# Gates and half of a convolution's columns taken out of the attention and projection stages and made 2x2 block products of seven

## The chip, the cores and the metric

One Trainium2 chip, one of its cores. The metric is the device time of one execution in microseconds (us); for the kernel before it is the median of three runs. The engines are named as in the profile: PE is TensorE (PEld its weight loads), DVE VectorE, ACT ScalarE, POOL GpSimd, SP the queue that issues nearly all DMAs.

## What is computed

One decoder layer over 1024 positions of width 1024, in float32. A normalised input h is multiplied by one wide matrix w_in; its columns feed three token mixers (an mLSTM with 4 heads, a gated convolution of width 3, a stick-breaking attention with 16 heads) and three sets of gate columns. Then follow projections, a sum under the gates, an output product and an MLP of width 4096.

```python
h = rmsnorm(x, norm_mix_g)
ml_q, ml_k, ml_v, ml_o, ml_i, ml_f, sc_b, sc_c, sc_u, sb_q, sb_k, sb_v, g_ml, g_sc, g_sb = split(h @ w_in)
y_ml = head_rmsnorm(sigmoid(ml_o) * mlstm(ml_q, ml_k, ml_v, ...), ml_norm_g)
y_sc = sc_b * causal_conv3(sc_c * sc_u, conv_w)
y_sb = stick_breaking(sb_q, sb_k, sb_v)   # a = sigmoid(z_ts) * prod_{s<j<t} (1 - sigmoid(z_tj))
merged = (sigmoid(g_ml) * (y_ml @ w_ml_proj) + sigmoid(g_sc) * (y_sc @ w_sc_proj)
          + sigmoid(g_sb) * (y_sb @ w_sb_proj))
x = x + merged @ w_out
x = x + square(relu(rmsnorm(x) @ w_up)) @ w_down
return rmsnorm(x)
```

## The kernel before

**Products.** Every large product is made of three matmuls (`mm3`, lines 129 to 132): each operand is split into a high and a low part (`split`, an ACT copy in line 136 and a DVE subtraction in line 137), and high x high, high x low and low x high are added up in a PSUM bank. `dense_ws` (line 159) gives 128 columns of h @ w for all 1024 positions: it loads 512 KB of weights into a tile `wr`, splits them (two ACT and two DVE instructions of 128x512), and issues 2 x 8 x 3 = 48 matmuls of 512 columns into two banks. `dense_as` (line 173) does the same with the positions as stationary operand and 256 columns: 192 matmuls.

**Stages.** (1) The normalised, transposed input `hT` is made, 16 pairs of high and low tiles of 128x512. (2) mLSTM: for each head `ml_proj` and `ml_attn`. (3) Attention: for p = 0 to 7 (two heads each), `sb_qk` (K and Q, two `dense_ws`), `sb_attn`, and `sc_unit(p)`, which is 128 columns of the convolution (three `dense_ws`: c, u, b); before each even p `sb_v` makes the values of a pair of p's (one `dense_as`). (4) `branch` three times: eight columns of 128 of a projection, each with a `gate` before it (a `dense_ws` with a sigmoid). (5) w_out. (6) The MLP, which already works with 2x2 blocks of seven products (Strassen-Winograd): the up stage takes 16 units of 84 matmuls each.

**Attention's chain.** For each of 24 tiles of scores in one p (12 of them 512 wide, four each 384, 256 and 128; 16 lie on the diagonal): two score matmuls (lines 556 and 557); two sigmoids on ACT (559, 560); on POOL, for the tile on the diagonal, two selects (564, 566), for others a copy (570); a running product on DVE, the scan (572); a product on POOL (573); transposes on PE (590); splits on ACT and DVE (136, 137); matmuls with the values (603 to 607); a copy and an add into the output (613, 614). The tiles come in four groups, G = 3 to 0, of 8, 8, 4 and 4. K of the next p needs tiles that this p gives back after G = 2 (line 620).

**Order.** A scheduler lays out each engine's queue when the program is built. `ml_attn` and `sb_attn` are marked as urgent (`tc.high_priority(offset=AHEAD)`); the `dense_ws` of the convolution, of the next K and Q and of the next values stand between attention's instructions wherever the scheduler finds the latter not ready. Each engine works through its queue in order.

The lines that the change touches most:

```python
    for p in range(8):                       # 687
        ...
        Q, T = sb_qk(p)
        with tc.high_priority(offset=AHEAD):
            sb_attn(p, Q, T, vt)
        ...
        sc_unit(p)                           # 695
```

Of the kernel before, what the change touches and what calls it, by code (L numbers as in the profile page):

```python
# [16 lines left out]
P = 128  # L17
# [17 lines left out]
AHEAD = 2000  # L35


@with_exitstack
def hybrid_block_kernel(
# [66 lines left out]
    def g(name):  # L106
        return rings[name].get()
# [517 lines left out]
    def sc_unit(ct):  # L625
        cs, zs = [None, None], [None, None]

        def ev_c(th, ps):
            cs[th] = g("sc")
            nc.scalar.activation(cs[th][:, :512], ps, AF.Copy)  # L630

        def ev_u(th, ps):
            z = g("sc")
            zs[th] = z
            if th == 0:
                nc.gpsimd.memset(z[:, 0:2], 0.0)
            else:
                nc.gpsimd.tensor_copy(z[:, 0:2], zs[0][:, 512:514])
            nc.vector.tensor_tensor(z[:, 2:514], cs[th][:, :512], ps, ALU.mult)
            t = cs[th]  # L640
            nc.vector.tensor_scalar(t[:, :512], z[:, 2:514], cw[:, 2, ct:ct + 1], None, ALU.mult)
            nc.vector.scalar_tensor_tensor(t[:, :512], z[:, 1:513], cw[:, 1, ct:ct + 1], t[:, :512], ALU.mult, ALU.add)
            nc.vector.scalar_tensor_tensor(t[:, :512], z[:, 0:512], cw[:, 0, ct:ct + 1], t[:, :512], ALU.mult, ALU.add)
            if th == 1:
                free(*zs)

        def ev_b(th, ps):
            t = cs[th]
            nc.vector.tensor_tensor(t[:, :512], t[:, :512], ps, ALU.mult)
            nc.sync.dma_start(ysc_d[ct][:, th * 512:(th + 1) * 512], t[:, :512])  # L650
            free(t)

        dense_ws(w_in, C_SCC + ct * P, hT, ev_c)
        dense_ws(w_in, C_SCU + ct * P, hT, ev_u)
        dense_ws(w_in, C_SCB + ct * P, hT, ev_b)
# [10 lines left out]
    def gate(c0, ct, ring=None):  # L666
        sg = [None, None]

        def ev_g(th, ps):
            sg[th] = (ring or ring_f).get()  # L670
            nc.scalar.activation(sg[th][:, :512], ps, AF.Sigmoid)
        dense_ws(w_in, c0 + ct * P, hT, ev_g)
        return sg
# [24 lines left out]
    unplan(ring_f, "u", "be", "yo", "avt", "sc")  # L698
    unplan(banks, "z", "av", "acc", "tp")
    plan(banks, acc=6, tp=2)  # L700

    def branch(i, w, c0, yd, sgs):
        y = [[None, None] for _ in range(KO)]
        nxt = len(sgs)
        for ko in range(KO):
            y[ko] = [(ring_r.get(), ring_r.get()) for _ in range(2)]
            load_split(yd[ko], 1, y[ko])
            if ko in (1, 3, 5) and nxt < (5 if i == 0 else 3):
                sgs[nxt] = gate(c0, nxt)
                nxt += 1  # L710
        for ct in range(KO):
            while nxt < min(KO, ct + 2):
                sgs[nxt] = gate(c0, nxt)
                nxt += 1
            if i == 2 and ct == KO - 1:
                free_all(hT)
            sg = sgs.pop(ct)

            def ev_p(th, ps):
                s = sg[th][:, :512]  # L720
                nc.vector.tensor_tensor(s, s, ps, ALU.mult)
                if i == 0:
# [403 lines left out]
```

## Time and profile before

| | |
|---|---|
| three runs | 2522.91 us median (2522.04 to 2523.82) |
| profiled execution | 2525.46 us, of it 2523.7 us span |
| busy | PE 98%, DVE 60%, ACT 44%, POOL 30% of the span |
| attention's scans (line 572) | first at 533.0 us, last at 1238.2 us |
| gates (line 671) | first sigmoid at 1222.4 us, last at 1738.9 us |
| products with the projections (line 721) | 1286.7 to 1761.2 us |
| output product (line 850) | 1782.8 to 1856.7 us |
| up stage (line 939) | 1874.3 to 2176.5 us |

A row of the timeline gives start, duration, engine, line, operation, output<-inputs and shape; "[0.95 <-POOL gf L570]" behind it says how long the engine had been idle and what released it. A row of groups ends in the number of instructions, busy time and mean duration. PE's matmuls are pipelined: one of 512 columns shows a duration of 397 ns, but the distance from one to the next is what counts.

### The profile page before, as it was taken

Reading aid. Unit: us, or ns where it says so; the run is one execution under the profiler, and the core shown is the slowest. Engines: PE = TensorE matmul, PEld = TensorE weight load, DVE = VectorE, ACT = ScalarE, POOL = GpSimd, SP = SyncE. Lnnn points to the kernel's source line nnn. Section 1 sums busy time; section 2 is a strip of 40 time slices with the busy share of each in tenths; the row PEclk is TensorE's granted clock in tenths of the full one; section 3 lists DMA queues with packets and bytes.
Section 4 is the critical chain, followed back from the end, with each engine's and each line's share of the span. In section 5 each row is a group of like instructions: output and inputs, shape, how many; then the busy total and the mean of one; then the engine's idle time right before and its main releaser. Section 6 shows DMA issues by size and latency. Waiting matters only on the chain.

```text
span 2523.7 us, 35184 instructions
## 1 busy us (share of the span) xinstructions
PE 2473.0 (98%) x12792; PEld 2086.4 (83%) x12792; DVE 1520.9 (60%) x2337; ACT 1115.0 (44%) x2270; POOL 751.7 (30%) x1108
## 2 busy tenths in 40 slices
PE   7999999999999999999999999999989999899998
PEld 6899898988888888888888888888868888678776
DVE  6465463767757767767621322424357677797996
ACT  6343333346546546546521311313446666643343
POOL 3000010034434334344300000000246565654563
PEclk9999999999999999999999999999999999999999
DMA  4121111122122122222221311312426665875663
GB/s 123 47 64 55 55 39 59 36 70 64 50 64 55 51 63 55 57 61 59 91 69 50 117 42 50 117 42 86 140 72 209 203 202 182 279 247 185 226 203 128
DMA packets 273637, 256.66 MB, mean 102 GB/s; under 512 B 20016, under 2 KB 224816, under 8 KB 273464
## 3 DMA queue, kind: packets, MB, share of 16 engines
q1 hardware_dynamic: 271016, 249.96, 31.7%
q10 hardware_dynamic: 2448, 4.46, 0.5%
q8 instruction: 100, 1.64, 0.3%
q14 instruction: 73, 0.60, 0.1%
HBM read 178.85 MB, written 67.13 MB: 97 GB/s over the span
## 4 chain that ended last, share of the span: by engine, by line
PE 89%; DVE 4%; POOL 2%; DMA 2%; issue 2%; ACT 1%; SPq 0%; POOLq 0%; DVEq 0%; ACTq 0%
PE ps L130 27%; PE ps L131 27%; PE ps L132 27%; PE ps L590 2%; DVE gr L137 1%; PE ps L557 1%; PE ps L556 1%; PE ps L607 1%; PE ps L606 1%; DVE gf L1081 1%; DMA gr<-gd 1%; DVE gf L572 1%; POOL gf L759 0%; DMA wr<-in_w_in_dram 0%; POOL gf L573 0%
## 5 line engine op out<-in xcount | busy, mean ns | idle before, releaser
L130 PE MATMUL ps<-gr,wh 128*128 128x512 f32 x1938 | 768.3, 397 | 7.5 <-ACT gf L939 6.7
L131 PE MATMUL ps<-gr,wh 128*128 128x512 f32 x1938 | 767.1, 396 | 0.0
L132 PE MATMUL ps<-gr,wl 128*128 128x512 f32 x1924 | 760.4, 396 | 0.0
L130 PEld LDWEIGHTS ps<-gr,wh 128*128 128x128 f32 x1938 | 365.0, 188 | 91.0 <-ACT gf L939 7.1
L131 PEld LDWEIGHTS ps<-gr,wh 128*128 128x128 f32 x1938 | 364.7, 188 | 83.3 <-DVE gr L137 0.6
L132 PEld LDWEIGHTS ps<-gr,wl 128*128 128x128 f32 x1924 | 362.0, 188 | 82.9
L137 DVE TENSOR_TENSOR wl<-wr,wh 128x512 fp32r<-128x512 f32 (+1 forms) x261 | 187.6, 726 | 302.1 <-ACT wh L136 297.7
L136 ACT ACTIVATE wh<-wr 128x512 fp32r<-128x512 f32 (+1 forms) x268 | 167.7, 631 | 434.7 <-PE ps L131 374.6
L130 PE MATMUL ps<-gr,gr 128*128 128x512 f32 (+3 forms) x730 | 261.1, 364 | 6.1 <-DVE gf L1081 5.8
L131 PE MATMUL ps<-gr,gr 128*128 128x512 f32 (+3 forms) x730 | 264.2, 364 | 0.0
L132 PE MATMUL ps<-gr,gr 128*128 128x512 f32 (+3 forms) x730 | 262.8, 364 | 0.6 <-DVE gr L1021 0.6
L572 DVE TENSOR_TENSOR_SCAN gf<-gf 128x512 f32<-128x512 f32 (+1 forms) x192 | 200.8, 1048 | 100.5 <-POOL gf L564 56.8
L137 DVE TENSOR_TENSOR gr<-gf,gr 128x512 fp32r<-128x512 f32 (+2 forms) x222 | 206.5, 942 | 62.9 <-ACT gr L136 58.8
L573 POOL TENSOR_TENSOR gf<-gf,gf 128x512 f32<-128x512 f32 (+1 forms) x192 | 185.3, 967 | 175.8 <-DVE gf L572 145.8
L130 PE MATMUL ps<-wh,gr 128*128 128x256 f32 (+2 forms) x792 | 229.3, 290 | 7.2 <-DVE gf L1081 4.1
L131 PE MATMUL ps<-wl,gr 128*128 128x256 f32 (+2 forms) x800 | 229.3, 287 | 0.0
L132 PE MATMUL ps<-wh,gr 128*128 128x256 f32 (+2 forms) x792 | 225.4, 288 | 0.2 <-DVE gr L140 0.2
L136 ACT ACTIVATE gr<-ps 128x256 fp32r<-128x256 f32 (+2 forms) x304 | 129.7, 442 | 170.7 <-PE ps L132 70.7
L759 POOL TENSOR_TENSOR gf<-wr,wr 128x512 f32<-128x512 f32 x22 | 34.6, 1572 | 563.6 <-PE ps L854 552.7
L759 POOL TENSOR_TENSOR gf<-gf,gf 128x512 f32<-128x512 f32 x106 | 152.5, 1445 | 118.8 <-ACT gf L953 90.1
L136 ACT ACTIVATE gr<-gf 128x512 fp32r<-128x512 f32 (+2 forms) x222 | 135.9, 622 | 109.6 <-POOL gf L759 71.8
L137 DVE TENSOR_TENSOR gr<-ps,gr 128x256 fp32r<-128x256 f32 (+2 forms) x304 | 142.7, 483 | 59.0 <-ACT gr L136 55.9
(204 smaller groups left out, 3969.6 us busy)
## 6 DMA issues: line engine op xcount, KB each, us to landing
wr<-in_w_in_dram SPq DMA_DIRECT2D x102, 512.0 KB, 3.7
gr<-gd SPq DMA_DIRECT2D x145, 256.0 KB, 5.1
gd<-gr SPq DMA_DIRECT2D x128, 256.0 KB, 2.5
wr<-in_w_down_dram SPq DMA_DIRECT2D x30, 512.0 KB, 5.2
gd<-gf SPq DMA_DIRECT2D x48, 256.0 KB, 2.6
gf<-in_w_up_dram SPq DMA_DIRECT2D x36, 256.0 KB, 3.0
gr<-gr SPq DMA_DIRECT2D x64, 128.0 KB, 2.2
gf<-in_x_dram SPq DMA_DIRECT2D x31, 256.0 KB, 3.7
```

Of the source, the lines that this page charges most:

```text
L130: mm(ps, lh, rh, start=start, stop=False, skip_group_check=chain)
L131: mm(ps, lh, rl, start=False, stop=False, skip_group_check=chain)
L132: mm(ps, ll, rh, start=False, stop=stop, skip_group_check=chain)
L136: nc.scalar.activation(hi, src, AF.Copy)
L137: nc.vector.tensor_tensor(lo, src, f32(hi), ALU.subtract)
L556: mm(ps[:, :w], qs, kx[ch][:, :w], start=True, stop=False)
L557: mm(ps[:, :w], qs, ky[ch][:, :w], start=False, stop=True)
L572: nc.vector.tensor_tensor_scan(ur, ur, ur, u[:, w:w + 1], ALU.mult, ALU.bypass)
L573: nc.gpsimd.tensor_tensor(be[:, :w], be[:, :w], u[:, 1:w + 1], ALU.mult)
L590: nc.tensor.transpose(pt[:, k * 256 + ti * P:k * 256 + (ti + 1) * P], blk, ident)
L606: mm(pav[:, 0:256], vs, ah[:, o], start=(s == ns - 2), stop=False)
L759: nc.gpsimd.tensor_tensor(dst[:, :512], a[:, :512], b[:, :512], op)
```

## The change

1. **Convolution.** `NSC = 4`: of the eight sets of 128 columns four stay in the attention stage. Their 12 `dense_ws` are spread over the eight p (`conv[len(conv) * p // 8 : ...]`: one for even p, two for odd p), where 24 stood before (three each).
2. **A new stage** stands behind attention: the other four sets of convolution columns (6 units) and all gates (12 units) as 2x2 blocks of seven products, 84 matmuls for 256 columns where two `dense_ws` took 96. A unit loads four weight blocks of 256 KB, makes four sums of them on POOL (`left`), splits seven operands (ACT and DVE), and evacuates seven products (ACT copies, DVE adds). Gates go to DRAM (`sg_d`) and are loaded again in `branch`.
3. **Sums of the input** that the block products need (16 tiles of 128x512) are made in the mLSTM stage: `sums_h`, 32 POOL instructions and 16 writes of 256 KB; behind attention they are loaded and split into the tiles that attention gives back.
4. **`branch`** has no gates in between any more; it loads y straight into the low tiles, without `wr`.

```diff
+    def sums_h(k, ring):
+        b11, b12, b21, b22 = [ring.get() for _ in range(4)]
+        for t, (hi, lo) in zip((b11, b12, b21, b22), (hT[k][0], hT[k][1], hT[4 + k][0], hT[4 + k][1])):
+            pool_tt(t, f32(hi), f32(lo), ALU.add)
+        for i, (d, p, q) in enumerate(((b11, b12, b11), (b12, b22, b12), (b22, b22, b11), (b21, b21, b22))):
+            pool_tt(d, p, q, ALU.subtract)
+            nc.sync.dma_start(t_d[i][k], d[:, :512])
+        free(b11, b12, b21, b22)
...
         with tc.high_priority(offset=AHEAD):
             ml_attn(h, st)
+        sums_h(h, rings["sc"])
...
+    conv = [u for ct in range(NSC) for u in sc_unit(ct)]
...
-        sc_unit(p)
-    sgs = {k: gate(C_GML, k, rings["sc"]) for k in range(2)}
+        for c0, ev in conv[len(conv) * p // 8:len(conv) * (p + 1) // 8]:
+            dense_ws(w_in, c0, hT, ev)
...
+    for i, d in ((3, 0), (2, 2), (4, 1), (6, 3)):
+        hB[i] = []
+        for k in range(4):
+            hi, lo = ring_r.get(), ring_r.get()
+            nc.sync.dma_start(f32(lo[:, :512]), t_d[d][k])
+            nc.scalar.activation(hi[:, :512], f32(lo[:, :512]), AF.Copy)
+            nc.vector.tensor_tensor(lo[:, :512], f32(lo[:, :512]), f32(hi[:, :512]), ALU.subtract)
+            hB[i].append((hi, lo))
...
+    def unit(c0, off=0, last=None):
+        a = blocks_load(w_in, c0, quarters.get)
+        parts, made = left(ring_f.get, a[0][0], a[0][1], a[1][0], a[1][1])
...
+        for i in ORDER:
+            wh, wl = w_part(wts, parts[i])
...
+            for k in range(4):
+                ks = slice(k * P, (k + 1) * P)
+                rh, rl = hB[i][k]
+                mm3(ps, wh[:, ks], wl[:, ks], rh[:, :512], rl[:, :512], FIRST[i] and k == 0, k == 3, True)
...
+    for ct in range(NSC, KO, 2):
+        conv_units(ct)
+    for b, c0 in enumerate((C_GML, C_GSC, C_GSB)):
+        for ct in range(0, KO, 2):
+            sg = unit(c0 + ct * P, 0, AF.Sigmoid)
...
-            while nxt < min(KO, ct + 2):
-                sgs[nxt] = gate(c0, nxt)
-                nxt += 1
...
+            sg = [ring_f.get() for _ in range(2)]
+            for th in range(2):
+                nc.sync.dma_start(sg[th][:, :512], sg_d[b][ct][th])
```

Line numbers of the kernel after stand one higher than before up to line 623. In the rows of an engine's order the figure behind a tile's name tells buffers apart.

PE in the attention of p = 0, some ten score tiles in, before (130 to 132 are the convolution's u, whose weights are `wh` and `wl`; 556 and 557 scores):

```order
L556 MATMUL ps_166<-gr_105,gr_97 128x256
L557 MATMUL ps_166<-gr_107,gr_97 128x256
L132 MATMUL ps_164<-gr_67,wl_158 128x512
L130 MATMUL ps_164<-gr_71,wh_153 128x512
L131 MATMUL ps_164<-gr_72,wh_153 128x512
L132 MATMUL ps_164<-gr_71,wl_158 128x512
L130 MATMUL ps_164<-gr_75,wh_153 128x512
L131 MATMUL ps_164<-gr_76,wh_153 128x512
L132 MATMUL ps_164<-gr_75,wl_158 128x512
L556 MATMUL ps_167<-gr_101,gr_97 128x512
L557 MATMUL ps_167<-gr_103,gr_97 128x512
```

The same scores on PE in the kernel after (557 and 558 are scores, 607 and 608 products with the values):

```order
L557 MATMUL ps_167<-gr_101,gr_97 128x512
L558 MATMUL ps_167<-gr_103,gr_97 128x512
L607 MATMUL ps_168<-gr_123,gr_116 128x256
L557 MATMUL ps_166<-gr_105,gr_97 128x128
L558 MATMUL ps_166<-gr_107,gr_97 128x128
L608 MATMUL ps_168<-gr_124,gr_116 128x256
L607 MATMUL ps_168<-gr_123,gr_115 128x256
L608 MATMUL ps_168<-gr_124,gr_115 128x256
L607 MATMUL ps_168<-gr_125,gr_118 128x256
L608 MATMUL ps_168<-gr_126,gr_118 128x256
L607 MATMUL ps_168<-gr_125,gr_117 128x256
L608 MATMUL ps_168<-gr_126,gr_117 128x256
```

The columns that stood between attention's matmuls are gone there: 64 rows of attention, with 10 tiles of scores, follow one another without one of `dense_ws`.

DVE at the same place before (572 is the scan; 639 to 643 the convolution; 137 with `wl<-wr` the split of its weights):

```order
L572 SCALAR_TENSOR_TENSOR gf_148<-gf_148 128x384
L639 TENSOR_TENSOR gf_146<-gf_144,ps_165 128x512
L137 TENSOR_TENSOR wl_157<-wr_150,wh_152 128x512
L641 TENSOR_SCALAR gf_144<-gf_146,cw 128x512
L572 SCALAR_TENSOR_TENSOR gf_149<-gf_149 128x512
L642 SCALAR_TENSOR_TENSOR gf_144<-gf_146,cw,gf_144 128x512
L137 TENSOR_TENSOR gr_126<-ps_163,gr_125 128x512
L643 SCALAR_TENSOR_TENSOR gf_144<-gf_146,cw,gf_144 128x512
L137 TENSOR_TENSOR gr_124<-ps_162,gr_123 128x512
L572 SCALAR_TENSOR_TENSOR gf_131<-gf_131 128x256
L572 SCALAR_TENSOR_TENSOR gf_135<-gf_135 128x512
```

And DVE in the kernel after, a few scans further on (573 is the scan, 138 the split of attention's weights, 615 the output add, 530 a part of the next K):

```order
L573 SCALAR_TENSOR_TENSOR gf_135<-gf_135 128x512
L573 SCALAR_TENSOR_TENSOR gf_137<-gf_137 128x512
L138 TENSOR_TENSOR gr_126<-ps_163,gr_125 128x512
L138 TENSOR_TENSOR gr_119<-ps_162,gr_119 128x128
L530 TENSOR_TENSOR gr_106<-ps_164,gr_110 64x512
L573 SCALAR_TENSOR_TENSOR gf_148<-gf_148 128x256
L573 SCALAR_TENSOR_TENSOR gf_131<-gf_131 128x128
L138 TENSOR_TENSOR gr_124<-ps_162,gr_123 128x512
L573 SCALAR_TENSOR_TENSOR gf_149<-gf_149 128x512
L573 SCALAR_TENSOR_TENSOR gf_135<-gf_135 128x512
```

The scans and attention's splits stand as before; the instructions of the convolution between them have left. Counted from the first to the last scan of one p, DVE's queue holds four splits of loaded weights where it held eight (even p) or six (odd p), and one set of 641 to 643 where it held two.

SP early in the mLSTM stage before (`mb` and `dec` belong to the mLSTM's gates):

```order
L147 DMA wr_151<-in_w_in_dram 128x8x128
L787 DMA gmlp<-in_norm_mlp_g_dram 128x8x1
L309 DMA mb_406<-gf_128 4x512
L371 DMA gf_133<-mb_406 128x512
L147 DMA wr_150<-in_w_in_dram 128x8x128
```

The same place after (`td` are the sums of the input):

```order
L148 DMA wr_151<-in_w_in_dram 128x8x128
L909 DMA gmlp<-in_norm_mlp_g_dram 128x8x1
L689 DMA td_3_415<-gf_143 128x512
L310 DMA mb_406<-gf_128 4x512
L689 DMA td_3_419<-gf_144 128x512
L372 DMA gf_133<-mb_406 128x512
L689 DMA td_3_423<-gf_146 128x512
L148 DMA wr_150<-in_w_in_dram 128x8x128
```

Writes that wait for POOL now stand ahead of loads of weights.

## Rows read from the trace of the kernel before

**Rows 1.** The page: span, and PE's busy time, share and instructions.

```profile
span 2523.7 us, 35184 instructions
PE 2473.0 (98%) x12792; PEld 2086.4 (83%) x12792; DVE 1520.9 (60%) x2337; ACT 1115.0 (44%) x2270; POOL 751.7 (30%) x1108
```

**Rows 2.** Windows: start:end, length, busy us (instructions) by engine, granted clock, DMA.

```profile
1300.00:1350.00 50.00, 50.00 (x217) 40.42 (x216) 11.38 (x17) 7.41 (x12) 0.00 (x0) 1.00 0.19 53
1950.00:2000.00 50.00, 50.00 (x217) 40.43 (x216) 34.39 (x36) 32.47 (x57) 30.12 (x21) 1.00 0.64 210
```

**Rows 3.** Waits of PE from 520 to 1260 us: total, times, longest.

```profile
PE ps L607 <- DVE gr L137: 3.0, 3, 1.0
```

**Rows 4.** Windows of one pair of p's (4 and 5), from first scan to first scan.

```profile
905.60:971.80 66.20, 66.20 (x355) 56.44 (x354) 52.72 (x72) 39.02 (x87) 39.41 (x81) 1.00 0.22 59
971.80:983.90 12.10, 12.10 (x60) 10.00 (x59) 6.94 (x17) 5.37 (x14) 0.71 (x2) 1.00 0.18 56
983.90:1045.40 61.50, 60.33 (x372) 53.16 (x371) 51.00 (x75) 37.08 (x87) 37.12 (x80) 1.00 0.14 42
1045.40:1092.70 47.30, 47.30 (x276) 41.31 (x276) 20.92 (x43) 18.03 (x38) 0.70 (x2) 1.00 0.29 76
```

**Rows 5.** DVE's timeline in p = 4: start, us, line, operation, tiles, idle before.

```profile
905.64 1.28 DVE L572 TENSOR_TENSOR_SCAN gf<-gf 128x512 f32<-128x512 f32 x1 [4.00 <-POOL gf L564]
...
919.26 0.46 DVE L641 TENSOR_SCALAR gf<-gf,cw 128x512 f32<-128x512 f32 x1
...
921.74 0.74 DVE L643 SCALAR_TENSOR_TENSOR gf<-gf,cw,gf 128x512 f32<-128x512 f32 x1
...
932.10 0.73 DVE L572 TENSOR_TENSOR_SCAN gf<-gf 128x256 f32<-128x256 f32 x1
...
937.09 0.47 DVE L572 TENSOR_TENSOR_SCAN gf<-gf 128x128 f32<-128x128 f32 x1
...
946.27 0.69 DVE L137 TENSOR_TENSOR wl<-wr,wh 128x512 fp32r<-128x512 f32 x1
...
954.20 1.02 DVE L572 TENSOR_TENSOR_SCAN gf<-gf 128x384 f32<-128x384 f32 x1 [0.37 <-POOL gf L564]
```

**Rows 6.** POOL's timeline in the same stretch.

```profile
943.10 0.64 POOL L573 TENSOR_TENSOR gf<-gf,gf 128x256 f32<-128x256 f32 x1 [0.69 <-DVE gf L572]
943.67 0.18 POOL L570 COPY gf<-gf 128x1 f32<-128x1 f32 x1
...
946.57 0.54 POOL L564 TENSOR_SCALAR_AFFINE_SELECT gf<-gf 128x128 f32<-128x128 f32 x1
947.07 0.29 POOL L566 TENSOR_SCALAR_AFFINE_SELECT gf<-gf 128x128 f32<-128x128 f32 x1
947.78 0.41 POOL L573 TENSOR_TENSOR gf<-gf,gf 128x128 f32<-128x128 f32 x1 [0.42 <-DVE gf L572]
...
952.83 1.09 POOL L573 TENSOR_TENSOR gf<-gf,gf 128x512 f32<-128x512 f32 x1 [1.23 <-DVE gf L572]
...
955.37 0.86 POOL L573 TENSOR_TENSOR gf<-gf,gf 128x384 f32<-128x384 f32 x1 [0.89 <-DVE gf L572]
```

**Rows 7.** Groups by shape, 500 to 1262 us: count | busy us, mean ns | idle before.

```profile
L564 POOL TENSOR_SCALAR_AFFINE_SELECT gf<-gf 128x128 f32<-128x128 f32 x128 | 55.5, 433 | 238.1 <-ACT gf L559 236.3 <-PE ps L132 1.6
...
L572 DVE TENSOR_TENSOR_SCAN gf<-gf 128x512 f32<-128x512 f32 x96 | 123.3, 1284 | 81.6 <-POOL gf L564 39.7 <-POOL gf L570 38.4 <-ACT wh L136 1.9
```

**Rows 8.** PE's timeline in a run of 256-column products of the values.

```profile
1051.19 0.28 PE L130 MATMUL ps<-wh,gr 128*128 128x256 f32 x1
...
1054.37 0.29 PE L130 MATMUL ps<-wh,gr 128*128 128x256 f32 x1
```

**Rows 9.** The page, groups: POOL's block sums of two tiles.

```profile
L759 POOL TENSOR_TENSOR gf<-gf,gf 128x512 f32<-128x512 f32 x106 | 152.5, 1445 | 118.8 <-ACT gf L953 90.1 <-DVE gr L137 12.7 <-ACT gf L856 11.9
```

**Rows 10.** Windows at the start of the up stage (granted clock: third figure from the end).

```profile
1868.00:1872.00 4.00, 0.25 (x2) 0.00 (x0) 4.00 (x6) 4.00 (x9) 1.63 (x2) 0.84 0.00 0
...
1876.00:1880.00 4.00, 4.00 (x10) 2.80 (x9) 4.00 (x5) 0.10 (x1) 2.69 (x3) 0.50 0.00 1
```

More of the change, by code (lines that the diff above doesn't have):

```diff
@@ L35 @@
 AHEAD = 2000
+NSC = 4
 @with_exitstack
@@ L622, in sb_attn, with move, pool_tt @@
         free(*[t[0] for t in Q + T])
+    BANK = (0, 2, 0, 1, 0, 1, 0)
+    FIRST = (True, True, False, True, False, False, False)
+    ORDER = (0, 3, 1, 2, 4, 5, 6)
+    def move(src, dst, n=None):
+        ts = [src.free.popleft() for _ in range(len(src.free) if n is None else n)]
+        for t in ts:
+            owner[id(t)] = dst
+        dst.tiles.extend(ts)
+        dst.free.extend(ts)
+        return ts
+    def pool_tt(dst, a, b, op):
+        nc.gpsimd.tensor_tensor(dst[:, :512], a[:, :512], b[:, :512], op)
@@ new lines, in blocks_load, with w_part @@
+    def blocks_load(w, c0, get):
+        a = [[None, None], [None, None]]
+        for k in range(2):
+            for n in range(2):
+                q = get()
+                a[n][k] = q
+                nc.sync.dma_start(q[:, :512].rearrange("p (k c) -> p k c", k=4),
+                                  w[k * 512:(k + 1) * 512, c0 + n * P:c0 + (n + 1) * P]
+                                  .rearrange("(k p) c -> p k c", p=P))
+        return a
+    def w_part(wts, src):
+        wh, wl = wts.get(), wts.get()
+        split(wh[:, :512], wl[:, :512], src[:, :512])
+        return wh, wl
@@ L664, in hybrid_block_kernel @@
     mhl = [[None, None] for _ in range(KO)]
[L666 to L673, printed above, removed]
+    sg_d = [[[dr.tile([P, 512], F32, tag=f"sg{b}_{i}_{t}", name=f"sg{b}_{i}_{t}") for t in range(2)] for i in range(KO)]
+            for b in range(3)]
     plan(banks, acc=2, z=2, av=2)
@@ new lines, in hybrid_block_kernel @@
+    quarters = Ring([t[:, o:o + 512] for t in ring_wr.tiles for o in (0, 528)], "q")
+    own_q = move(ring_f, quarters, 4)
+    wts = Ring(ring_wh.tiles + ring_wl.tiles, "wts")
+    for k in range(4):
+        free(*hT[k][1])
+    own_w = move(ring_r, wts)
+    def unit(c0, off=0, last=None):
+        a = blocks_load(w_in, c0, quarters.get)
+        parts, made = left(ring_f.get, a[0][0], a[0][1], a[1][0], a[1][1])
+        bank = [None] * 3
+        s = {}
+        o = slice(off, off + 512)
+        for i in ORDER:
+            wh, wl = w_part(wts, parts[i])
+            if FIRST[i]:
+                bank[BANK[i]] = g("p")
+            ps = bank[BANK[i]]
+            for k in range(4):
+                ks = slice(k * P, (k + 1) * P)
+                rh, rl = hB[i][k]
+                mm3(ps, wh[:, ks], wl[:, ks], rh[:, :512], rl[:, :512], FIRST[i] and k == 0, k == 3, True)
+            free(wh, wl)
+            if i in (0, 2, 3):
+                s[i] = ring_f.get()
+                nc.scalar.activation(s[i][:, o], ps, AF.Copy)
+            elif i == 6:
+                s[6] = ring_f.get()
+                nc.scalar.activation(s[6][:, o], ps, last or AF.Copy)
+                free(ps)
+            else:
+                j = {1: 0, 4: 3, 5: 2}[i]
+                nc.vector.tensor_tensor(s[j][:, o], s[j][:, o], ps, ALU.add)
+                if i != 4:
+                    free(ps)
+        free(*made, *[q for r in a for q in r])
+        return [[s[0], s[2]], [s[6], s[3]]]
@@ new lines, in conv_units @@
+    def conv_units(ct):
+        cs = unit(C_SCC + ct * P, 2)
+        us = unit(C_SCU + ct * P)
+        for n in range(2):
+            for th in range(2):
+                z, t = cs[n][th], us[n][th][:, :512]
+                if th == 0:
+                    nc.gpsimd.memset(z[:, 0:2], 0.0)
+                else:
+                    nc.gpsimd.tensor_copy(z[:, 0:2], cs[n][0][:, 512:514])
+                nc.vector.tensor_tensor(z[:, 2:514], z[:, 2:514], t, ALU.mult)
+                nc.vector.tensor_scalar(t, z[:, 2:514], cw[:, 2, ct + n:ct + n + 1], None, ALU.mult)
+                nc.vector.scalar_tensor_tensor(t, z[:, 1:513], cw[:, 1, ct + n:ct + n + 1], t, ALU.mult, ALU.add)
+                nc.vector.scalar_tensor_tensor(t, z[:, 0:512], cw[:, 0, ct + n:ct + n + 1], t, ALU.mult, ALU.add)
+            free(*cs[n])
+        bs = unit(C_SCB + ct * P)
+        for n in range(2):
+            for th in range(2):
+                t = bs[n][th][:, :512]
+                nc.gpsimd.tensor_tensor(t, t, us[n][th][:, :512], ALU.mult)
+                nc.sync.dma_start(ysc_d[ct + n][:, th * 512:(th + 1) * 512], t)
+            free(*us[n], *bs[n])
@@ L700, in hybrid_block_kernel, with branch @@
+    for t in own_w:
+        wts.free.remove(t)
+        owner[id(t)] = ring_r
+        ring_r.free.append(t)
+    for t in own_q:
+        quarters.free.remove(t)
+        owner[id(t)] = ring_f
+        ring_f.free.append(t)
+    ring_wh = Ring(ring_wh.tiles, "wh")
+    ring_wl = Ring(ring_wl.tiles, "wl")
+    unplan(banks, "p")
     plan(banks, acc=6, tp=2)
-    def branch(i, w, c0, yd, sgs):
-        y = [[None, None] for _ in range(KO)]
-        nxt = len(sgs)
+    def branch(b, w, yd):
+        y = []
@@ L705, in branch @@
         for ko in range(KO):
-            y[ko] = [(ring_r.get(), ring_r.get()) for _ in range(2)]
-            load_split(yd[ko], 1, y[ko])
-            if ko in (1, 3, 5) and nxt < (5 if i == 0 else 3):
-                sgs[nxt] = gate(c0, nxt)
-                nxt += 1
-        for ct in range(KO):
-            while nxt < min(KO, ct + 2):
[L713 to L717, printed above, removed]
+            y.append([(ring_r.get(), ring_r.get()) for _ in range(2)])
@@ L927, in hybrid_block_kernel @@
         for i in ORDER:
-            wh, wl = first[i] if u == 0 and i < 5 else w_part(parts[i])
+            wh, wl = first[i] if u == 0 and i < 5 else w_part(wts, parts[i])
             if FIRST[i]:
```

95 lines of the change are left out of this document (43 added, 52 removed).

## The prediction

> **What bounds the kernel now.** I began with the page: PE is busy for 98% of the span [rows 1]. A busy PE isn't yet a PE at its peak, so the next view was that of the windows, in two stages that differ much: gates and projections, where the other engines idle, and the block products of the up stage, where POOL works for 30 us of 50, DVE for 34 and ACT for 32 [rows 2]. In both PE gets through 217 matmuls of 512 columns in 50 us, 0.2304 us each, at the full clock. A block unit of 84 matmuls thus takes 19.4 us and is bound by PE. Attention came third: its largest wait on PE adds up to 3.0 us from 520 to 1260 us [rows 3]. On this reading everything is bound by PE's columns, and a change that takes columns away should be faster.
>
> That reading says what PE does now, not what attention could do without the columns that fill it. So I took one pair of p's, 4 and 5, apart, in four windows: 66.2 us from the first scan to the last of p = 4, 12.1 to the next first scan, 61.5 for p = 5, and a tail of 47.3 in which the values' and the next K's products run, 187.1 us in all [rows 4]. DVE is busy for 52.7 of the 66.2 and POOL for 39.4. Together that is more than the window: do they work side by side, or in turn? The timelines answer. A scan of 512 takes 1.28 us, of 384 1.02, of 256 0.73, of 128 0.47; a split of loaded weights takes 0.69, and the convolution's lines 641 and 643 take 0.46 and 0.74, with 642 taken as 643 [rows 5]. POOL's product takes 1.09, 0.86, 0.64 and 0.41 for the four widths and starts when a scan has ended; a select takes 0.29 us, but 0.54 while the weight split of 946.27 to 946.96 runs on DVE, and a copy takes 0.18 [rows 6]. Over all of attention the first select averages 0.433 us, and the scans of 512 stand idle for 81.6 us, 78 of it behind POOL's selects and copies [rows 7].
>
> So I added up one p as if nothing of these ran side by side. Scans: 12 x 1.28 + 4 x 1.02 + 4 x 0.73 + 4 x 0.47 = 24.2 us. POOL's products: 12 x 1.09 + 4 x 0.86 + 4 x 0.64 + 4 x 0.41 = 20.7. Selects 32 x 0.29 = 9.3, copies 8 x 0.18 = 1.4. That makes 55.6, of attention alone. Beside it DVE's queue holds, in an even p, eight weight splits (5.5) and two sets of 641 to 643 (2 x 1.94 = 3.9): 65.0 where 66.2 was measured. In an odd p six splits make it 63.6, measured 61.5. The pair: 128.6 against 127.7, a ratio of 0.993. **DVE and POOL taken in turn explain attention's pace as well as PE's columns do**; the columns fill a pace that is there without them.
>
> **The change part by part.** *Columns.* 18 units of 84 matmuls stand where 36 sets of 48 stood: 1728 - 1512 = 216 fewer, 49.8 us if PE stayed busy. But they also move. By the order, the products of 512 columns between attention's first and last score go from 1855 to 1248: 607 fewer, 139.9 us of PE. After the last score they go from 5321 to 5712: 391 more, 90.1 us. The second is paid in full, since units and projections run at PE's pace [rows 2]. The first is a gain only as far as attention shrinks.
>
> *Attention's pairs.* By the order one p keeps four weight splits (2.8 us) and one set of 641 to 643 (1.9): 55.6 + 4.7 = 60.3, the pair 120.6, and by the ratio of before 119.8 instead of 127.7: 7.9 us less. The 12.1 between stays. In the tail the values' products of 256 columns shrink, as the queue now finds room for them earlier: by the order 140 of them stand between a pair's last score and the next pair's first, and then 51 in two places and 76 in the third. From 1051.19 to 1054.37 us 28 of them begin [rows 8], 0.118 us apart, so 89 fewer are 10.5 us and 64 fewer 7.5. I put the tail at 38 us rather than 36.8, as K's parts and the first scores of the next p remain in it. The pair becomes 119.8 + 12.1 + 38 = 169.9, or 17.2 less; the third 14.4 less; three pairs 48.8. In the last pair no next values are in the tail, and splits of the new sums (seven of 0.69) and two block sums come into DVE's and POOL's turn instead: I take 0.5 less. Attention: -49 us, and not -140.
>
> The Trainium skill ("SBUF — State Buffer", section "Who interferes with whom") says that a DVE instruction with two inputs in SBUF contends with a POOL instruction that reads SBUF, and that the one that comes second fully blocks. By that rule without the ratio of 0.993 the pair would be 170.7, the sum 2 us higher; were it wrong, PE's pace would hold, which is the first rival. The select that takes 0.54 us instead of 0.29 beside a weight split agrees with it.
>
> *The sums in the mLSTM stage.* 32 POOL instructions of 1.445 us [rows 9], 46 us, beside a POOL that is little used there; they read tiles that DVE's splits need too. 16 writes of 256 KB stand on SP ahead of weight loads and wait for POOL, so behind each a `wr` load can be late, and PE behind that. The trace has no such write; bounds 0 and 8 us; I take 2, as weights are loaded well ahead.
>
> *Entry into the units.* 16 loads, ACT copies and DVE subtractions into tiles that attention gives back; bounds 0 (all beside the last p) and 15 us (the whole tail of attention without columns behind it); I take 3. *Exit, and projections without gates.* y is loaded into tiles of the last unit as they come free, gate tiles are read back from DRAM: 48 matmuls of a column are 11.1 us for a weight load of 512 KB, and DMA has a share of 0.19 in that stage [rows 2]. Hidden, 0. POOL's and DVE's share of a unit is the up stage's [rows 2]: hidden behind PE, nothing.
>
> The sum on the span: 2523.7 - 49 + 90 + 5 = 2569.7, or +46. The profiled execution is 2.6 us over the median of the runs and has 1.8 us around its span; I carry the difference over to the median: 2522.9 + 46 = **2569 us**.
>
> **The rivals.** *Attention goes at PE's pace* (faster). The chain's pace was set by columns and follows when they go: 2523.7 - 140 + 90 + 5 = 2479, some 2478 on the median. The pair would be 154 us. For it: PE has almost no wait there [rows 3], and DVE by itself would need less. Against it: 55.6 us per p of scans and POOL's work in turn leaves 111 of the pair's 154 before one split, and POOL's products begin at the ends of scans. The point from which the sum turns: attention must shrink by 95 us instead of 49, which is a pair of about 157. Chance 0.13.
>
> *DVE and POOL overlap in part* (slower, by less). With odd p's at 61.5 against 63.6 some of the turns do lie side by side. Were each p 57 us instead of 60, eight of them would give 24 more back: 2545; at 54 us it is 2521. Chance 0.2, of which 0.02 at its low end.
>
> *Idle PE lowers the clock* (slower, by more). Ahead of the up stage PE is idle for most of 1868 to 1872, and from 1876 to 1880 the granted clock is 0.50, half of 2.4 GHz, and 10 matmuls run where 17 fit [rows 10]: about 1.7 us for one fall. If PE, which then waits in every p, has one fall in each and two more at attention's ends, ten make +17: 2586. Chance 0.12. The Trainium skill ("TensorE: Matmul & The Clock Gate", Part 1) calls the low level the default that activity releases; these rows agree.
>
> That the change does not do what it says is excluded: the order has the 216 fewer.
>
> **How the numbers follow.** Forecast with its small terms 0.49, overlap 0.2, clock 0.12, entry and SP at their upper bounds (18 more) 0.03, PE's pace 0.13, a pair between the two paces at the point where the sum turns 0.03. The range goes from 2520, the low end of the overlap, to 2594, the clock's case with half of the late loads; below it lie PE's pace and little else. 0.2% is 5 us, about what a measurement of this kernel can tell from no change: faster 0.13 (PE's pace), same 0.05 (the turn and the overlap's low end), slower 0.82 (the rest).
>
> **What would show it.** In the profile of the changed kernel: a pair of p's of about 170 us from first scan to first scan (154 for PE's pace); PE below 100% in attention, with tens of us of waits behind attention's splits and sigmoids; scans of 1.28 us and POOL products of 1.09 that still take turns; units of 19.4 us with 217 matmuls in 50 us at the full clock; gates and units from attention's end on some 90 us longer than before. It would be wrong if PE's waits in attention stayed at a few us, or if the stage behind attention grew by clearly more than 95 us.

## The result and the profile after

The changed kernel takes 2588.02 us (median of four runs, 2583.08 to 2592.09) against 2522.84 us (median of four) for the kernel before: a ratio of 1.0251, interval 1.0237 to 1.0266. It is 65 us slower; 46 were forecast, inside a range of -3 to +71. The profiled execution takes 2592.09 us, 2590.4 of it span. Three points that exist in both traces (attention's first and last scan, and the last product with a projection) divide the 66.7 us of span into four stretches:

| stretch | before | after | difference | forecast |
|---|---|---|---|---|
| start to attention's first scan | 533.0 | 539.8 | +6.8 | +2 |
| first scan to last scan | 705.2 | 662.7 | -42.5 | -49 |
| last scan to last product with a projection (721, now 880) | 523.0 | 623.5 | +100.5 | +93 |
| from there to the end | 762.5 | 764.4 | +1.9 | 0 |

The scans of the changed kernel (first and last start), and its page, which answers to [rows 1]:

```profile
L573 DVE TENSOR_TENSOR_SCAN gf<-gf x192: 453/1268/2202, 539.8 to 1202.5; 128x512 f32<-128x512 f32 x96, 128x384 f32<-128x384 f32 x32, 128x256 f32<-128x256 f32 x32, 128x128 f32<-128x128 f32 x32
```

```profile
span 2590.4 us, 35588 instructions
PE 2467.0 (95%) x12576; PEld 2070.6 (80%) x12576; DVE 1642.1 (63%) x2453; ACT 1183.3 (46%) x2392; POOL 932.8 (36%) x1220
```

PE is busy for only 6 us less, though it has 216 products fewer, and its share of the span has fallen from 98 to 95%. The windows of the new stage (columns as in [rows 2]) show the block units at the pace of before:

```profile
1240.00:1290.00 50.00, 50.00 (x217) 40.47 (x217) 30.03 (x40) 16.14 (x28) 25.49 (x20) 1.00 0.31 86
...
1390.00:1440.00 50.00, 50.00 (x217) 40.52 (x216) 19.30 (x27) 21.79 (x37) 14.50 (x11) 1.00 0.37 109
```

So it is in attention that the saving is lost. Here is its whole stretch as one window, of the kernel before:

```profile
533.00:1238.20 705.20, 701.75 (x3940) 605.30 (x3939) 508.49 (x779) 382.72 (x849) 308.43 (x649) 1.00 0.21 57
```

and of the changed kernel, with PE's waits there (answering to [rows 3]):

```profile
539.80:1202.50 662.70, 594.90 (x3312) 509.28 (x3311) 484.23 (x716) 362.11 (x817) 327.63 (x646) 0.95 0.18 50
```

```profile
PE ps L604 <- DVE gr L138: 29.7, 20, 2.2
PE ps L557 <- ACT gf L561: 10.9, 14, 1.7
PE ps L591 <- DVE gr L138: 10.4, 10, 2.0
PE ps L591 <- POOL gf L574: 4.3, 3, 2.3
...
PE ps L131 <- DVE gr L138: 3.5, 4, 1.5
```

The groups by shape count 2053 products of 512 columns in that stretch before and 1428 after: 625 fewer, worth 144.0 us at 0.2304. PE's waits between the two scans add up to 3.4 us before and 67.4 after: 64 given back, most of it where a product with the values (604) or a transpose (591) waits for DVE's split. The granted clock is 1.00 before and 0.95 after: it stands at 0.50 for 61 of the 662.7 us, so 31 us of work are lost to it. -144 + 64 + 31 = -49, measured -42.5; another 6.5 us came back that neither explains. **Of 144 us of columns about 95 came back as waits and as a lower clock.**

The windows of a pair of p's, the second, answer to [rows 4] (p = 2, p = 3, the tail; 12.7 us lie between the first two):

```profile
714.93:772.30 57.37, 52.40 (x274) 43.87 (x273) 46.84 (x61) 33.60 (x79) 41.23 (x79) 0.97 0.16 40
784.99:843.42 58.43, 52.30 (x362) 47.04 (x361) 49.67 (x73) 35.62 (x85) 37.60 (x79) 1.00 0.10 30
```

```profile
843.42:890.16 46.74, 42.18 (x213) 35.66 (x212) 20.33 (x42) 18.62 (x38) 0.70 (x2) 0.93 0.30 76
```

The pair takes 175.2 us, not 169.9. Each p is shorter than forecast (57 and 58, not 60), and the tail is hardly shorter (46.7, where 38 was forecast and 47.3 stood before). In it the values' products of 256 columns did fall, from 119 to 48, which is 8.4 us at 0.118. But the 124 products of 512 columns stay, eight more of attention's own lie there, PE waits 4.6 us, and the clock of 0.93 costs 3.3.

### The profile page after: what moved, and what is told of

Read it like the earlier page. It is cut to its first block, busy times and chain, and to the rows that moved or that the text cites. A ratio compares the mean times of both kernels' runs of the same rounds, so it can differ in the third digit from the quotient of the medians.

```text
span 2590.4 us, 35588 instructions
## 1 busy us (share of the span) xinstructions
PE 2467.0 (95%) x12576; PEld 2070.6 (80%) x12576; DVE 1642.1 (63%) x2453; ACT 1183.3 (46%) x2392; POOL 932.8 (36%) x1220
## 5 line engine op out<-in xcount | busy, mean ns | idle before, releaser
L131 PE MATMUL ps<-gr,wh 128*128 128x512 f32 x1530 | 609.1, 398 | 11.1 <-ACT gf L1044 6.7
L132 PE MATMUL ps<-gr,wh 128*128 128x512 f32 x1530 | 606.8, 397 | 1.6 <-DVE gr L772 1.3
L133 PE MATMUL ps<-gr,wl 128*128 128x512 f32 x1516 | 599.6, 397 | 0.0
L131 PE MATMUL ps<-gr,gr 128*128 128x512 f32 (+3 forms) x954 | 349.3, 371 | 6.6 <-DVE gf L1186 5.9
L131 PEld LDWEIGHTS ps<-gr,wh 128*128 128x128 f32 x1530 | 289.6, 189 | 79.2 <-ACT gf L1044 7.1
L132 PE MATMUL ps<-gr,gr 128*128 128x512 f32 (+3 forms) x954 | 352.6, 371 | 0.0
L133 PE MATMUL ps<-gr,gr 128*128 128x512 f32 (+3 forms) x954 | 350.6, 371 | 0.7 <-DVE gr L1126 0.6
L132 PEld LDWEIGHTS ps<-gr,wh 128*128 128x128 f32 x1530 | 289.3, 189 | 68.3 <-DVE gr L772 1.8
L133 PEld LDWEIGHTS ps<-gr,wl 128*128 128x128 f32 x1516 | 286.0, 189 | 66.4
L645 POOL TENSOR_TENSOR gf<-gf,gf 128x512 f32<-128x512 f32 x158 | 225.9, 1436 | 210.1 <-ACT gf L1058 88.3
L138 DVE TENSOR_TENSOR wl<-wr,wh 128x512 fp32r<-128x512 f32 (+1 forms) x192 | 145.7, 766 | 141.1 <-ACT wh L137 133.8
L574 POOL TENSOR_TENSOR gf<-gf,gf 128x512 f32<-128x512 f32 (+2 forms) x192 | 185.4, 969 | 103.6 <-DVE gf L573 80.2
L131 PEld LDWEIGHTS ps<-gr,gr 128*128 128x128 f32 x954 | 179.8, 189 | 43.9 <-DVE gf L1186 8.9
L137 ACT ACTIVATE gr<-ps 128x512 fp32r<-128x512 f32 (+2 forms) x304 | 131.5, 445 | 178.7 <-PE ps L133 66.9
L133 PEld LDWEIGHTS ps<-gr,gr 128*128 128x128 f32 x954 | 180.1, 189 | 33.9 <-DVE gr L1126 1.1
```

The lines of the kernel that those rows point to most:

```text
L131: mm(ps, lh, rh, start=start, stop=False, skip_group_check=chain)
L132: mm(ps, lh, rl, start=False, stop=False, skip_group_check=chain)
L133: mm(ps, ll, rh, start=False, stop=stop, skip_group_check=chain)
L137: nc.scalar.activation(hi, src, AF.Copy)
L138: nc.vector.tensor_tensor(lo, src, f32(hi), ALU.subtract)
L574: nc.gpsimd.tensor_tensor(be[:, :w], be[:, :w], u[:, 1:w + 1], ALU.mult)
```

## The experiments

A set is here one `dense_ws`, 48 products of 512 columns or 11.1 us of PE; attention holds 24 of the convolution's before, 12 after the change.

**Only the gates as units.** All 24 sets return to attention.

```diff
-NSC = 4
+NSC = 8
```

> All 24 sets of convolution columns go back into attention (six each pair of p's) and only the gates are block units. Theory (attention is held at 56 to 58 us per p by DVE's and POOL's turns and at 48 us per tail, so columns taken out of it give little back, and columns put into it cost little): first to last scan some 705 us as before, 43 more than the changed kernel's 662.7, while 6 units of 19.4 us (116 us) leave the stage behind it. 2588 + 43 - 116 = 2515, less the 5 to 10 us of waits at the units' entry: 2500 to 2515, faster than the kernel before by 0.3 to 0.9%. Rival (the units, their sums and their entry are what costs, wherever columns stand): the gates' units keep the 7 us ahead of the first scan and 12 us behind the last, and the stage is no faster than before: 2520 to 2545.

Measured: 2515.99 us, ratio 0.9971 (0.9959 to 0.9982), 1 us above the theory's range and below the rival's. Attention as one window:

```profile
539.20:1239.80 700.60, 691.12 (x3874) 595.60 (x3873) 512.52 (x778) 382.17 (x848) 313.32 (x650) 1.00 0.21 58
```

It takes 700.6 us from first to last scan, at a clock of 1.00 and with 9.4 us of waits. Twelve sets more, 133 us of PE, thus lengthen it by 38 us; as units behind attention the same columns cost 115 us. Against the kernel before, the gates' units save 144 products, worth 33 us. Of these 61 are missing between the first and the last scan, which is only 4.5 us shorter, and 83 (19 us) behind it, where the rest of the kernel is 12.6 us shorter and PE waits 5.7 us longer.

**K and Q ahead of the values.**

```diff
-        if p % 2 == 0:
-            vt = sb_v(p // 2)
         Q, T = sb_qk(p)
+        if p % 2 == 0:
+            vt = sb_v(p // 2)
```

> The changed kernel with K and Q of an even p written ahead of the pair's values, so that they can stand in the p before as they do for odd p's. Theory A (the tail of 48 us between pairs is an order: the values' products need tiles that come free at the pair's end, and K and Q, 96 products of 512 columns, 22 us, queue behind them): the tail falls from 48 to some 25 us as PE has idle time in the p before; three tails, -60 to -70 us, 2520 to 2530. Theory B (the tail is bound by the values' own columns and by attention's last splits): K and Q move but the values then take their place; tail 40 to 48, 2565 to 2590.

Measured: 2539.09 us, ratio 1.006 (1.0043 to 1.0077): 49 us less than the changed kernel, with the same work. The gap between pairs falls from 47 to 9, 12 and 12 us, the one inside a pair grows from 13 to 24 to 30. No product of the values stands in the latter: mostly K and Q of the odd p do, with 79 to 103 products of 512 columns where 37 to 47 stood. A p takes 61 to 64 us but for the first (72), the second pair 160.1. The last scan comes 52 us earlier, 33 of them ahead of attention: the first scan is at 506.8 and not at 539.8, as the first values are made behind it. Between first and last scan attention is 18.6 us shorter. The windows of two p's (2 and 4) and of the whole attention:

```profile
681.97:743.70 61.73, 60.47 (x401) 54.98 (x400) 50.43 (x76) 38.55 (x92) 39.16 (x77) 1.00 0.14 39
842.09:903.80 61.71, 60.39 (x401) 54.96 (x400) 50.42 (x76) 38.55 (x92) 39.12 (x77) 1.00 0.14 39
506.77:1150.90 644.13, 612.03 (x3553) 535.04 (x3552) 505.71 (x745) 373.34 (x843) 316.12 (x646) 0.97 0.20 55
```

The values now fill the even p's (157 of the 401 products in each of these windows), K and Q the odd ones; PE is 60 of 62 us busy, and waits fall from 67 to 32 us. The length of the tail was a matter of order, as theory A had it. The gain is 49 and not 60 to 70, as most p's grow by 3 to 6 us, the first by 16, and about half of what the tails lost is back inside the pairs.

**More work for DVE, of two kinds.** In the attention stage (`extra` has one entry there and none elsewhere), behind each split of loaded weights, two more instructions:

```diff
+            for _ in range(2 * len(extra)):
+                nc.vector.tensor_tensor(lo[:, :w], raw[:, i * w:(i + 1) * w], f32(hi[:, :w]), ALU.subtract)
```

> The changed kernel with each DVE split of loaded weights in the attention stage made three times over (the same result): two more DVE instructions of 128x512 with two SBUF inputs, 0.69 us each, eight per p between its first and last scan. Theory (DVE and POOL take turns; their union fills 54 to 56 of a p's 56 to 58 us): the eight cost their 5.5 us in full, 57 becomes 62.5 per p, 2588 + 44 = 2632, and something more in tails. Rival (DVE is busy for 46 to 50 of 57 us and has room): +0 to 15, 2588 to 2603.

```diff
+            for _ in range(2 * len(extra)):
+                nc.vector.tensor_reduce(dmy, raw[:, i * w:(i + 1) * w], mybir.AxisListType.X, ALU.add)
```

> At the same places two DVE sums over 512 elements (one SBUF input, one element out for each partition) instead of the two subtractions; its time on DVE is not in any trace, taken as 0.5 to 0.7 us. Theory (turns are between a DVE instruction with two SBUF inputs and a POOL instruction): these run beside POOL's, so they cost less than half of what the subtractions cost: 2588 to 2610, and their own duration does not stretch beside POOL's products. Rival (it is DVE's own order that holds attention up, whatever the instruction reads): the same cost per us of DVE as with the subtractions.

Measured: 2642.56 us with the subtractions (+54.5 on the changed kernel), 2622.63 with the sums (+34.6), above the theory's 2588 to 2610 for these. Attention grows by 49.9 and 31.7 us. In the first kernel its window, the instructions (minimum/median/maximum in ns) and one of PE's waits:

```profile
543.50:1256.10 712.60, 617.73 (x3311) 528.60 (x3310) 571.49 (x834) 366.04 (x817) 335.09 (x647) 0.92 0.17 46
L155 DVE TENSOR_TENSOR wl<-wr,wh x144: 657/686/1470, 446.2 to 1183.7; 128x512 fp32r<-128x512 f32 x144
PE ps L132 <- DVE wl L155: 12.8, 3, 4.3
```

and in the second its window, the instructions and one of DVE's waits:

```profile
537.90:1232.30 694.40, 611.32 (x3312) 517.86 (x3311) 549.76 (x829) 366.15 (x817) 315.21 (x646) 0.94 0.17 47
L155 DVE TENSOR_REDUCE dmy<-wr x144: 627/686/689, 431.6 to 1107.2; 128x1 f32<-128x512 f32 x144
DVE dmy L155 <- DMA wr<-in_w_in_dram: 19.1, 18, 1.8
```

Both have a median of 0.686 us, 99 us for 144. The one with two SBUF inputs is stretched to as much as 1.47 us: 24 of the 144 take over 0.70, and beside each of these POOL runs its product of attention. One such place, a pair of the added subtractions on DVE (the first of them takes 1.47) and POOL at the same time, where the select takes 0.74 us and not 0.29:

```profile
548.18 2.19 DVE L155 TENSOR_TENSOR wl<-wr,wh 128x512 fp32r<-128x512 f32 x2
```

```profile
547.73 1.37 POOL L578 TENSOR_TENSOR gf<-gf,gf 128x512 f32<-128x512 f32 x1 [1.42 <-ACT wh L137]
549.06 0.74 POOL L569 TENSOR_SCALAR_AFFINE_SELECT gf<-gf 128x128 f32<-128x128 f32 x1
```

The sum with a single input never goes beyond 0.689, though 48 of the 144 lie beside a POOL instruction. So turns exist. The 18 us between the two kernels are not their price alone: the added subtractions write `wl` anew, and PE waits 12.8 us for that, which the sums don't ask of it. The sums cost 32 us without being stretched, which speaks for the rival, DVE's own place in the order; but part of that is DVE idle at them for 19.1 us until weights land, so the shares are not shown.

**POOL's product cut to one column.**

```diff
-                        nc.gpsimd.tensor_tensor(be[:, :w], be[:, :w], u[:, 1:w + 1], ALU.mult)
+                        nc.gpsimd.tensor_tensor(be[:, 0:1], be[:, 0:1], u[:, 1:2], ALU.mult)
```

> The changed kernel with POOL's product in attention cut to one column of each tile (the scans' weights are left without the product by the rest), so that POOL's 1.09 us for 512 columns is nearly gone: some 20 us per p by the sum of the turns. Theory (DVE and POOL take turns, their union fills 55 of 57 us per p): a p falls from 57 to PE's pace, which is busy for 52 of 57, and PE's waits in the scans' stretch go: 50 to 53 us per p, -30 to -45 in all, 2545 to 2558; the tails of 47 to 48 stay. Rival (the pace is the chain of ACT, selects and scans, or DVE's own order with POOL's product beside it): 2580 to 2590.

Measured: 2596.52 us, ratio 1.0284 (1.027 to 1.0298); no faster at all. The kernel leaves the product out of all other columns. Attention as one window:

```profile
540.27:1203.50 663.23, 596.08 (x3301) 511.52 (x3300) 449.29 (x717) 361.90 (x817) 185.84 (x645) 0.95 0.18 49
```

POOL is busy for 142 us less and DVE for 35 less than in the changed kernel, and attention takes 663.2 us instead of 662.7, with the same waits (66.6 us) and the same clock. The stretching is gone (scans of 512 columns average 1.280 us, where the changed kernel has 1.385), and still a p takes 59 to 61 us, where 50 to 53 were expected. My theory, that the sum of DVE's and POOL's turns sets the pace, finds no support here; the rival's range is missed too, by 6.5 us. One reservation: the scheduler laid PE's queue anew for the shorter instruction, so it isn't the same order with less POOL work, and such a run was not made.

**Weight splits' subtractions on POOL.**

```diff
-            split(hi[:, :w], lo[:, :w], raw[:, i * w:(i + 1) * w])
+            if extra:
+                nc.scalar.activation(hi[:, :w], raw[:, i * w:(i + 1) * w], AF.Copy)
+                nc.gpsimd.tensor_tensor(lo[:, :w], raw[:, i * w:(i + 1) * w], f32(hi[:, :w]), ALU.subtract)
+            else:
+                split(hi[:, :w], lo[:, :w], raw[:, i * w:(i + 1) * w])
```

> The changed kernel with the subtraction of each split of loaded weights in the attention stage on POOL instead of DVE (72 of them, the same result). Theory A (PE's waits in attention end at DVE's splits, so DVE's time is what counts, and POOL's does not, as the run with the short product suggests): 72 x 0.69 = 50 us leave DVE; by the run with doubled splits, 50 us longer for 99 us of DVE, attention gets some 25 us shorter: 2560 to 2575. Theory B (DVE and POOL in turn): POOL's instruction of two inputs takes 1.1 to 1.45 us, so the turns get 30 to 55 us longer, and selects queue behind them: 2600 to 2630.

Measured: 2632.39 us, ratio 1.0433 (1.0417 to 1.0449), 44 above the changed kernel. The moved instruction on POOL (count | busy, mean ns | idle before), and attention as one window:

```profile
L155 POOL TENSOR_TENSOR wl<-wr,wh 128x512 fp32r<-128x512 f32 x67 | 90.7, 1359 | 138.1 <-ACT wh L154 138.0
```

```profile
537.50:1242.60 705.10, 615.96 (x3312) 523.17 (x3311) 467.70 (x658) 364.78 (x817) 390.69 (x705) 0.92 0.17 46
```

Theory B comes near, 2 us above its range: a subtraction takes 1.36 us on POOL where DVE took 0.69, which over 72 is 48 us, and attention grows by 42. PE's waits rise to 88 us. More work on POOL lengthened attention in this run, though DVE had less, while less work on POOL didn't shorten it in the run above.

**The sums of the input in other places.** First written two heads later in the code:

```diff
-        sums_h(h, rings["sc"])
+        for k in {3: (), 0: (0,), 1: (1,), 2: (2, 3)}[h]:
+            sums_h(k, rings["sc"])
```

> The changed kernel with the sums of the first head's turn made two heads' turns later (none after the first head, two after the last), so that no POOL sum stands in the first 100 us. Theory (the first scan is 6.8 us later than before since POOL's sums delay what the mLSTM's gates wait for there): first scan back at some 533 to 534 us, 2588 - 6 = 2582. Rival (it is the writes on SP ahead of weight loads, which stay in number, or the lower clock of a single execution): no change, 2586 to 2590, first scan at 539.

Measured: 2589.13 us, first scan at 540.4. It decided nothing: the scheduler drew the sums ahead again, and their 16 writes stand between 50 and 98 us, in the changed kernel between 48 and 97. Then in tiles of the mLSTM's own ring (`rings["ft"]` for `rings["sc"]` in the same lines), which come free later:

> The changed kernel with the sums of the input made in tiles of the mLSTM's own ring, none in the first head's turn, so that they can't start before those tiles come free (in the run with the sums written later, all 16 writes still stood between 50 and 98 us, as the scheduler had drawn them ahead; it could tell nothing on their place). Theory (sums between 38 and 98 us delay POOL's selects and the gates' chain of the first head, and PE with it): first scan at 533 to 535 instead of 539.8, 2588 - 6 = 2582. Rival (SP's writes, or the tiles that the mLSTM lends): first scan at 538 or later, 2586 to 2594.

Measured: 2584.80 us (2583.13 to 2586.68), first scan at 535.9: 3.9 of the 6.8 us gone. What the sums did is to be seen on POOL, in the changed kernel (timeline, columns as in [rows 6]; 382 and 384 are the selects of the mLSTM):

```profile
53.49 2.66 POOL L645 TENSOR_TENSOR gf<-gf,gf 128x512 f32<-128x512 f32 x2
56.10 3.43 POOL L645 TENSOR_TENSOR gf<-gr,gr 128x512 f32<-128x512 f32 x2
59.48 0.86 POOL L382 TENSOR_SCALAR_AFFINE_SELECT gf<-gf 128x256 f32<-128x256 f32 x1
```

and in the kernel before at the same step:

```profile
55.22 0.40 POOL L381 TENSOR_SCALAR_AFFINE_SELECT gf<-gf 128x256 f32<-128x256 f32 x1 [3.04 <-DMA gf<-mb]
```

The select comes 4 us later, behind four sums. SP's writes have little part in it: from 15 to 85 us ACT waits 3.3 us for loaded weights where it waited 2.7. PE's clock there is 0.92 in the changed kernel and 1.00 before. But it is also 1.00 in the two runs that add DVE's sums or move subtractions to POOL, with the same sums of the input, and their first scans are at 537.9 and 537.5; so the clock is about 2 of the 6.8 us. The changed kernel, then the run with DVE's sums:

```profile
20.00:80.00 60.00, 51.84 (x306) 44.67 (x307) 45.93 (x87) 35.94 (x67) 44.58 (x35) 0.92 0.30 86
```

```profile
20.00:80.00 60.00, 49.98 (x319) 42.78 (x318) 46.39 (x88) 36.67 (x70) 45.38 (x35) 1.00 0.31 87
```

**Only gates as units, with the sums moved.** The first kind of move, and then the second:

> Only the gates as block units (all convolution columns in attention) and the sums delayed as in the run beside it. If the two gains stand apart: 2516 - 6 = 2510, 0.5% below the kernel before. If the sums only move the delay to a later head: 2516.

> Only the gates as block units, all convolution columns in attention, and the sums as in the run beside it. If the 6 us ahead of attention go: 2510. If they stay: 2516.

Measured: 2516.49 us, as without the move, and 2512.12 us, ratio 0.9948 (0.9935 to 0.996). The second is the fastest of this study, 12 us ahead of the kernel before.

**Columns spread otherwise.** Between the two ends, with 18 of the 24 sets in attention (`NSC = 6`), K and Q first, and the sums as in the first kind:

> Six sets of convolution columns in attention and one pair as units, sums delayed, K and Q ahead of the pair's values. From the run with K and Q first (2539, four sets in attention): three units fewer, -58 us behind attention; six sets of 48 more in it, 66 us of PE, of which PE's idle time there, some 25 to 30 us by the windows, takes a part; sums -6. Theory (PE's columns and DVE's and POOL's turns are near balance there): 2539 - 58 + 40 - 6 = 2515, 2508 to 2522. If the added weight splits and convolution lines cost their turns on top: 2530 to 2540.

Measured: 2544.16 us, ratio 1.0074 (1.0059 to 1.009), above both ranges; missed. The six sets more lengthen attention by 60 of their 66 us (704.4 from 644.1): with K and Q first PE had only 32 us of waits, and none of them went. And with all 24 in attention, the sums as in the second kind, but three sets, one each of p = 0, 2 and 4, moved to the last p:

```diff
-        for c0, ev in conv[len(conv) * p // 8:len(conv) * (p + 1) // 8]:
+        for c0, ev in conv[18 * p // 7:18 * (p + 1) // 7] if p < 7 else conv[18:]:
```

> The run with only the gates as units and the sums in the mLSTM's own tiles (2512), with the 24 sets of convolution columns spread otherwise: 18 over the first seven p's (two or three each) and six at the last p, where three stood. There the last pair of the 2512 run loses 13 us to PE's waits and some 9 us to a lower clock, between 1212 and 1272 us. Theory (columns are what attention's end lacks, and a pair that is short of three to six of 48 products is still at PE's pace or within a few us of the turns): 2512 - 5 to 15 = 2497 to 2507. Rival (the earlier p's are already at DVE's and POOL's turns, so that the columns moved out of them give nothing back there): 2512 to 2520.

Measured: 2516.43 us, 4 slower than without; inside the rival's range, though the first three pairs of p's do give 9 us back for 33 us of columns. The largest waits of PE in attention and at the entry of the units, before this move and after it:

```profile
PE ps L131 <- ACT wh L137: 3.8, 2, 3.0
PE ps L604 <- DVE gr L138: 3.6, 4, 2.4
```

```profile
PE ps L604 <- DVE gr L138: 13.1, 8, 2.1
```

One set less in each of three p's is enough for PE to wait 19 us in the first three pairs, where it waited 3.4. The waits of 12 us at attention's end, which the move was made for, are gone. In the kernel before, PE's pace and that of attention's chain lie that close together.

## Why the prediction was right, and where not

- *The gain of attention, and not of columns.* Right, the step on which the sign rests: 607 products, 140 us, were counted as 49 us of gain, and 42.5 came. It was also why the first reading of the page, PE bound everywhere, misled: a window in which PE is busy all the time says nothing on what lies just under it.
- *Why.* Half right. The forecast had DVE's and POOL's turns as the pace, on the sum of 65.0 us against 66.2 measured [rows 5, 6]. The stretched subtractions, and scans of 512 columns at 1.385 us in the changed kernel (1.284 before [rows 7]), show that there are turns. But a p took 56 to 59 us (the last 67) where the turns were to hold it at 60, and with 142 us less of POOL's work attention took the same time. The sum also counted only 33.6 us of scans, weight splits and convolution among the 52.7 us that DVE was busy in that p [rows 4]; the other 19, attention's own splits and adds, were left out without a row that showed them beside POOL. So the agreement of 0.993 was in part chance; PE's columns had the same pace. What the traces show in its place is the wait of PE at the head of its own queue: products with the values wait for DVE's split, PE waits 67 us in all, and what stands behind waits too. In which proportion ACT, DVE's place in the order and PE's queue make those waits is not settled; K and Q ahead of the values halve them at the same work, so the order is a large part.
- *The tail.* The step that failed: 38 us forecast, 46.7 to 48.0 measured. I subtracted 89 products and held the rest as it was, as if PE set the tail's length. 71 of them did go from the tail shown, and waits and a lower clock took their place. The length was set by an order, K and Q behind the values; with that turned round it is 9 to 12 us (and 11 to 18 more inside a pair). The p's erred the other way (12.8 us less per pair where 7.9 were forecast), and the stretch between two p's of a pair grew by 1 us, so the pairs' sum was 34.5 us less in place of 48.8; the last pair gave 7.9 more, where 0.5 was taken. That the total of attention, 42.5, came near the 49 is thus in part luck: errors of both signs met in it.
- *Overlap in part, the slower rival.* Its condition held, p's of about 57 us, and its time, 2545, did not: what the p's gave went back in tails that stayed long and in the clock.
- *The clock as a rival.* Priced at 17 us for ten falls of 1.7 [rows 10], given 0.12; it came beside the forecast and not in its stead, and belonged in the sum. The number of falls was near: in the changed kernel's attention the granted clock stands at 0.50, its lower level, in eleven stretches, 61 us together, 31 us lost. The price of one was too small, 1.7 us where these cost 2.8 on average. It was read from a single window, and the windows on both sides of it show the same fall:

```profile
1872.00:1876.00 4.00, 1.06 (x3) 0.87 (x4) 4.00 (x5) 2.14 (x5) 2.59 (x2) 0.50 0.00 0
1880.00:1884.00 4.00, 4.00 (x16) 2.92 (x14) 4.00 (x6) 0.60 (x1) 1.19 (x1) 0.88 0.44 130
```

PE works at half speed for 1.06 us of the first, for the 4 us of [rows 10] and for about 1 us of the last: 3 us lost. One of the two longest in attention, across the tail behind p = 1 of the changed kernel:

```profile
671.00:681.00 10.00, 8.21 (x38) 7.81 (x38) 4.59 (x12) 3.83 (x10) 0.00 (x0) 0.50 0.08 28
```

- *Behind attention.* 90.1 us for 391 products: right in kind, the units run at 217 in 50 us. From the last scan, by the trace, it is 416 products, 95.9 us, and 4.2 us of waits at the entry (3 taken), 100.1 of the 100.5. That is over the 95 us that the prediction set as a sign of being wrong, but the 391 were counted from the last score: from there (1232.7 us before, 1201.5 after) the stage grew by 95.9 us.
- *The sums.* 2 us taken, bounds 0 and 8; 6.8 measured, by what the trace shows mostly through POOL's select behind four sums and not through SP's writes as the step had it. Making them in later tiles gave 3.9 back.
- *PE's pace, the faster rival.* Ruled out: 175 us for a pair, not 154.

## What to carry to other kernels

Columns that fill an engine's queue beside a long chain are priced by what the chain would do without them, not by their own time; here 133 us of them cost attention 38, and 115 where they were moved to. Before such work is moved, look for the second limit just under the busy engine, and test it by taking a little away: one set of 11 us from each of three p's made PE wait. A saving of products belongs where PE is bound alone, which were the gates: that part by itself gained 0.3%, and 0.5% with the sums made later.

## What the runs showed of the hardware

A DVE sum over 512 elements with one SBUF input took 0.627 to 0.689 us in all 144 places, 48 of them beside a POOL instruction; a subtraction of two SBUF inputs at the same places took 0.657 to 1.470 us, and each of the 24 over 0.70 us lay beside a POOL product. That is what the Trainium skill ("SBUF — State Buffer", section "Who interferes with whom") says of both: two inputs in SBUF contend with POOL's reads, and a reduction never does. Not expected was how low the clock stood in a stage in which PE waits often and briefly: 0.95 over 662.7 us with waits of at most 3.0 us each, 67 us in all, and 0.92 with 88 and 94 us of them.
